# Two pairs of projections side by side in a hybrid attention, retention and linear-attention trunk

## The chip, the cores and the metric

The kernel runs on one core of a Trainium2 chip. The metric is the device time of one execution in microseconds; a kernel's time is the median of its runs. The core has five engines with instruction streams of their own: TensorE (PE; its weight loads are shown as PEld), VectorE (DVE), ScalarE (ACT), GpSimd (POOL) and SyncE (SP), which here only issues DMAs. Each runs its instructions in order and waits on semaphores for the others.

## The reference, cut to what matters

Two layers over 1024 tokens of width 1024, all in float32. A layer normalises the tokens, projects them once, runs three groups of heads beside each other, gates them and projects back:

```python
h = rms_norm(x, pre_gain) * (1.0 + scale) + shift
proj = h @ w_in
(aq, ak, av, ag, rq, rk, rv, rg, gq, gk, gv, gg, ga) = jnp.split(proj, IN_SPLITS, axis=-1)
...
a_out = sliding_window_attention(aq, ak, av, sinks) * jax.nn.silu(ag)
...
rq = apply_rotary(rq.reshape(B, S, RET_HEADS, RET_DK), positions, ret_freq)
rk = apply_rotary(rk.reshape(B, S, RET_HEADS, RET_DK), positions, ret_freq)
r = retention(rq, rk, rv.reshape(B, S, RET_HEADS, RET_DV))
r_out = rms_norm(r).reshape(B, S, RET_W) * jax.nn.silu(rg)
...
g = gated_linear_attention(...)
g_out = rms_norm(g, gla_norm_gain).reshape(B, S, GLA_W) * jax.nn.silu(gg)
y = jnp.concatenate([a_out, r_out, g_out], axis=-1) @ w_out
return x + gate * rms_norm(y, post_gain)
```

`rq`, `rk`, `rv` and `gv` are 256 columns wide each; `ak` and `av` are 128 each and lie next to each other, so the kernel treats them as one unit, `kv`, of 256.

## The kernel before, in words

**Tiles.** The tokens are eight tiles of 128; two tiles make a pair `p` (0 to 3), four a half `hf`. The columns of `w_in` and `w_out` are cut into units of 256 (`UNITS`): `gg` and `rg` (gates), `rq`, `rk`, `rv` (retention), `gqk` and `gv` (linear attention's queries with keys, and its values), `kv` (attention's keys and values), `aq0`, `aq1`, `ag0`, `ag1`, and `o0` to `o3` of the output.

**Precision.** Every float32 operand of a large product is held as two parts, a high part and the rest (`a` = 0 and 1). A product is three passes of eight matmuls over the 1024 rows (`PASSES`, L623; `accum`, L625): high by high, low by high, high by low. A projection of one tile by one unit is so 24 matmuls.

**Two shapes of projection.** `project` (L634) keeps a block of 128 tokens stationary and moves the 256 columns of one weight unit. `project_T` (L641) keeps 128 columns of weights stationary and moves 512 tokens, out of two pairs' token blocks that lie in two slots; the operand is made by `both` (L148), which describes two runs of 256 with one step between them. `y_half` (L1221) uses `both` for two weight units of the output in the same way.

**Memory.** Seven slots hold weights and token blocks in turn. `PLACE` (L53) says which unit goes to which slot in each layer, `TURNED` (L48) which units begin 48 elements into their slot, and `SW` (L51) where the blocks of layer 1's output product go. `load` (L520) fetches a unit in four chunks of 256 KB, one DMA each on SP's queue, into one of five staging buffers (`st`), and turns each chunk into its two parts: the high part by ACT or DVE, the rest by DVE, the last chunk's by POOL. A slot is written only when its last reader has finished. Other pools that matter below: eight 256-wide work tiles (`t1`), ten 512-wide ones (`t2`), two large ones (`mx`), three PSUM banks for projections (`mm`) and five for the rest (`aux`).

**The order of PE's work** is the order in which the program writes it. Projections are the trunk of that order. Everything else (cores of the heads, norms, the next layer's modulation) is written as jobs that yield a delay. The program keeps a planned clock, `clk`, which each matmul advances by its columns divided by 2400 (in us); between projections and inside `accum` it calls `pump`, which writes the steps of the jobs whose delay has passed. The delays are in the table `L` (L1691; a key with `@1` holds for layer 1): `rc1`, for example, is the time from a retention core's creation to its first transposes on PE. The other engines' order is left to the compiler's scheduler.

**The stages around the change.** In `layer` (L1480), after the gates, retention goes pair by pair: `rq` for two tiles, `rk` for two, `rv` for two. Each `rq` and `rk` tile is rotated by `ret_rot` (L1168), five DVE operations in `rotary` (L831) and one for the decay; each `rv` tile is evicted by ACT and creates its `ret_core` (L1174). A core transposes queries and keys on PE, evicts them by ACT, makes the scores, masks them on DVE, multiplies with the values and updates the state. After the last tile of each of these units, its slot's next unit is requested. Then comes linear attention: `gqk` in four units, `gv` pair by pair, each pair creating a `gla_core` (L1092), and `kv`, whose first pair stands between `gv`'s third and fourth pair and whose other pairs come after. `attn_kv` (L863) evicts the values and rotates and transposes the keys. Then follow attention's queries (`aq0`, `aq1`, with `attn_rot`, L875) and its gates (`ag0`, `ag1`).

The `pk`, `pm` of these functions are one `mm` bank each; a unit of 256 columns fills half of it.

Of the kernel before, what the change touches and what calls it, by code (L numbers as in the profile page):

```python
# [17 lines left out]
P = 128  # L18
# [29 lines left out]
TURNED = ("gqk", "aq0", "aq1", "ag0", "ag1")  # L48
TOKEN_AT, PLAIN_AT, TURNED_AT, OUT_AT, BLOCK_AT = 48, 0, 48, 0, 64
PLAIN = 2  # L50
SW = dict(W00=6, T1=3, W11=4, W10=5, T2=2, T3=0, T4=1)  # L51
TOK = ((1, 2, 3, 4), (3, 4, 0, 1))
PLACE = []  # L53
for _t, _w in zip(TOK, (0, 2)):
    PLACE.append(dict(gg=_w, rg=5, rq=6, rk=_w, rv=5, gqk=6, gv=_w, kv=5, aq0=6, aq1=_w, ag0=5, ag1=_w,
                      o0=_t[0], o1=_t[1], o2=5, o3=6))
# [37 lines left out]
def trunk(ctx: ExitStack, tc: tile.TileContext, ins, cst, out):  # L94
# [53 lines left out]
    def both(x, y):  # L148

        return bass.AP(x.tensor, x.offset, [x.ap[0], (y.offset - x.offset, 2), (1, 256)])  # L150
# [1329 lines left out]
    def layer(l):  # L1480
# [3 lines left out]
        def do_gates(name, p):  # L1484
            w = used(l, name)
            for t in (2 * p, 2 * p + 1):
                pg = mm()
                if name == "gg":
                    project(pg[:, 0:272], l, t, w, 272)
                    job(gla_logits(l, t, pg[:, 0:256], pg[:, 256:272]))  # L1490
                else:
                    project(pg[:, 0:256], l, t, w)
                    dma("ssr", srS[t], silu2(pg[:, 0:256]))
                pump()
            if p == NP_ - 1:
# [59 lines left out]
        def do_gv(p):  # L1555
            for t in (2 * p, 2 * p + 1):
                pm = mm()
                project(pm[:, 0:256], l, t, used(l, "gv"))
# [4 lines left out]
                pump()  # L1563
            if p == NP_ - 1:
                load(l, "aq1")

        def do_kv(p):
            if p == 0:
                new_kv()
            for t in (2 * p, 2 * p + 1):  # L1570
                pk = mm()
                project(pk[:, 0:256], l, t, used(l, "kv"))
                job(attn_kv(l, t, pk))
                pump()
# [116 lines left out]
L = {"sw1": 0.4, "ld1": 1.2, "ld2": 1.2, "ld1@1": 1.2, "ld2@1": 1.27, "swW00": 0.0, "swT1": 0.0, "swW11": 0.4, "swW10": 0.5, "tt1": 8.0, "tt2": 1.75, "tb1": 24.5, "tb2": 0.75, "pf3": 13.2, "pf1": 6.35, "pf2": 4.16, "mod1": 4.6, "mod2": 4.0, "mod3": 13.29, "mod4": 7.04, "mod5": 3.36, "mod6": 9.04, "pre1": 7.44, "kv1": 3.1, "kv2": 2.11, "aq1": 6.0, "aq7": 6.0, "ag1": 5.44, "aq2": 2.4, "aq6": 5.2, "aq3": 10.21, "aq4": 7.36, "aq5": 3.6, "hn1": 8.93, "hn2": 2.85, "gz1": 11.18, "gz2": 8.13, "gl1": 2.76, "gd3": 15.9, "gc1": 0.62, "gc2": 1.94, "gc3": 1.33, "gc4": 0.87, "gc6": 0.86, "gc5": 1.14, "rc1": 0.8, "rc2": 1.09, "rc3": 5.87, "rc4": 2.51, "fin1": 7.28, "lay1": 1.13, "gc4@1": 0.93, "mod2@1": 4.0, "mod3@1": 15.1, "mod5@1": 3.36, "mod6@1": 4.11, "pre1@1": 7.44, "kv1@1": 2.79, "kv2@1": 5.28, "aq1@1": 4.8, "aq7@1": 5.28, "ag1@1": 6.25, "aq2@1": 0.82, "aq6@1": 6.0, "aq3@1": 10.9, "aq4@1": 4.4, "aq5@1": 5.15, "hn1@1": 8.12, "hn2@1": 2.85, "gz1@1": 15.91, "gz2@1": 10.94, "gl1@1": 4.6, "gd3@1": 15.9, "gc1@1": 0.48, "gc2@1": 1.94, "gc3@1": 1.33, "gc6@1": 0.86, "gc5@1": 1.04, "rc1@1": 0.37, "rc2@1": 0.84, "rc3@1": 1.9, "rc4@1": 2.79, "fin1@1": 4.28, "lay1@1": 1.7}  # L1691
# [36 lines left out]
```

## Time and profile before

| | |
|---|---|
| runs | 1002.62, 1007.8 and 1005.75 us, median 1005.75 |
| profiled execution | 1000.26 us |
| its span, first to last instruction | 998.5 us |
| mean granted clock of TensorE | 0.987 of full |
| weights loaded out of `w_in` | 96 chunks of 256 KB |
| transposes on PE (L188), tiles of the work pool | 288 of 128 x 128 |

A page of the profile gives busy time by engine, the chain of waits that ended last, and groups of equal instructions by line and shape. In the timeline a row reads: start, length, engine, line, operation, output<-input, shapes, count; in square brackets stands how long the engine was idle before it and what ended that. A line of a helper stands for all its callers: L173 is every matmul, L188 every transpose, L157 every ACT copy, L162 most DMAs, L546 the low part of a weight chunk. `arena` is the memory of the slots. The end of a matmul is modelled; the start of the next one is what counts.

### The profile page before, as it was taken

Reading aid. Unit: us, or ns where it says so; the run is one execution under the profiler, and the core shown is the slowest. Engines: PE = TensorE matmul, PEld = TensorE weight load, DVE = VectorE, ACT = ScalarE, POOL = GpSimd, SP = SyncE. Lnnn points to the kernel's source line nnn. Section 1 sums busy time; section 2 is a strip of 40 time slices with the busy share of each in tenths; the row PEclk is TensorE's granted clock in tenths of the full one; section 3 lists DMA queues with packets and bytes.
Section 4 is the critical chain, followed back from the end, with each engine's and each line's share of the span. In section 5 each row is a group of like instructions: output and inputs, shape, how many; then the busy total and the mean of one; then the engine's idle time right before and its main releaser. Section 6 shows DMA issues by size and latency. Waiting matters only on the chain.

```text
span 998.5 us, 19629 instructions
## 1 busy us (share of the span) xinstructions
PE 961.3 (96%) x7133; PEld 825.5 (83%) x7133; DVE 690.5 (69%) x1698; ACT 409.6 (41%) x1152; POOL 236.0 (24%) x275
## 2 busy tenths in 40 slices
PE   5798999999999999999999999999999999999896
PEld 2598999888998777778889999998899877777675
DVE  3779856857767778664588285685666577676886
ACT  2476411324332556542356242123333267664231
POOL 2210101232330234330113010113332034555000
PEclk8899999999999999999999999999999999999998
DMA  9832613523326255668646151343132433487883
GB/s 315 296 114 79 186 48 88 161 89 101 110 81 188 79 154 155 203 192 259 228 150 203 49 175 38 106 136 116 41 107 85 127 90 123 131 247 242 262 268 136
DMA packets 129968, 148.76 MB, mean 149 GB/s; under 512 B 14112, under 2 KB 94284, under 8 KB 129872
## 3 DMA queue, kind: packets, MB, share of 16 engines
q1 hardware_dynamic: 124176, 137.96, 45.2%
q10 hardware_dynamic: 5696, 9.56, 2.5%
q8 instruction: 56, 0.92, 0.4%
q14 instruction: 40, 0.33, 0.1%
HBM read 109.20 MB, written 36.18 MB: 146 GB/s over the span
## 4 chain that ended last, share of the span: by engine, by line
PE 75%; DVE 10%; DMA 7%; ACT 3%; issue 3%; POOL 2%; SPq 1%; ACTq 0%; POOLq 0%; DVEq 0%
PE mm L173 56%; PE aux L173 14%; PE aux L188 4%; DMA st<-in_w_in_dram 2%; POOL sm L650 2%; DMA t<-mixF 1%; DMA xk<-in_x_dram 1%; DMA t<-in_x_dram 1%; DMA aoS<-t 1%; DMA a<-mixS 1%; DVE arena L546 1%; DVE arena L723 1%; ACT t L666 1%; DVE t L715 1%; SPq L162 1%
## 5 line engine op out<-in xcount | busy, mean ns | idle before, releaser
L173 PE MATMUL mm<-arena 128*128 128x256 f32 (+2 forms) x1824 | 299.5, 318 | 4.2 <-DVE t L1008 2.7
L173 PE MATMUL mm<-arena,arena 128*128 128x256 f32 (+2 forms) x1824 | 297.4, 316 | 0.3 <-DVE t L1008 0.3
L173 PEld LDWEIGHTS mm<-arena 128*128 128x128 f32 x1824 | 255.3, 191 | 28.4 <-issue 3.3
L173 PEld LDWEIGHTS mm<-arena,arena 128*128 128x128 f32 x1824 | 252.5, 188 | 23.9 <-issue 4.3
L650 POOL TENSOR_TENSOR sm<-sm,mhalf 128x1 f32<-128x1 f32 (+1 forms) x64 | 55.9, 874 | 347.3 <-DVE sm L649 334.9
L173 PE MATMUL mm<-arena,mx 128*128 128x512 f32 (+1 forms) x564 | 128.2, 383 | 1.4 <-ACT kept L1355 1.4
L173 PEld LDWEIGHTS mm<-arena,mx 128*128 128x128 f32 x564 | 101.6, 188 | 22.9 <-ACT kept L1355 1.8
L157 ACT ACTIVATE t<-aux 128x256 f32<-128x256 f32 (+2 forms) x124 | 55.9, 468 | 73.7 <-PE aux L188 62.5
L157 ACT ACTIVATE arena<-st 128x512 fp32r<-128x512 f32 x94 | 55.9, 626 | 51.2 <-PE mm L173 19.0
L546 POOL TENSOR_TENSOR arena<-st,arena 128x512 fp32r<-128x512 f32 x31 | 43.3, 1401 | 133.2 <-ACT arena L157 96.7
L945 POOL TENSOR_TENSOR smx<-smx,sm 128x512 f32<-128x512 f32 x32 | 36.4, 1138 | 124.2 <-DVE sm L944 114.2
L546 DVE TENSOR_TENSOR arena<-st,arena 128x512 fp32r<-128x512 f32 x77 | 59.1, 787 | 5.9 <-ACT arena L157 3.7
L941 ACT ACTIVATE smx<-smx,sm 128x129 f32<-128x129 f32 x128 | 49.9, 392 | 27.8 <-DVE sm L938 27.8
L188 PE MATMUL aux<-c_ident,t 128*128 128x128 f32 (+1 forms) x292 | 48.6, 284 | 7.8 <-DVE t L681 7.4
L375 DVE SCALAR_TENSOR_TENSOR acc<-st,c_act,acc 128x512 f32<-128x512 f32 x60 | 45.4, 757 | 14.1 <-DMA st<-in_w_mod_dram 13.6
L188 PEld LDWEIGHTS aux<-c_ident,t 128*128 128x128 f32 (+1 forms) x292 | 35.2, 145 | 15.0 <-DVE t L681 9.4
L989 ACT ACTIVATE t<-aux 128x256 f32<-128x256 f32 x32 | 12.3, 384 | 75.7 <-PE aux L173 72.2
L173 PEld LDWEIGHTS aux<-t,mx 32*128 32x128 f32 (+1 forms) x896 | 39.5, 187 | 3.8 <-issue 2.0
L713 ACT ACTIVATE t<-aux,mod,mod 128x128 f32<-128x128 f32 x68 | 25.7, 459 | 37.0 <-DVE t L1262 19.4
L173 PE MATMUL aux<-t,mx 32*128 32x32 f32 (+1 forms) x896 | 40.6, 272 | 0.0
L936 DVE COPY_PREDICATED smx<-c_curmask,aux 128x256 f32<-128x256 int32 x64 | 25.5, 447 | 16.0 <-ACT smx L157 13.0
L1262 DVE SCALAR_TENSOR_TENSOR t<-t,sm,t 128x512 f32<-128x512 f32 x32 | 24.0, 780 | 17.8 <-DMA t<-in_x_dram 11.5
(223 smaller groups left out, 1382.9 us busy)
## 6 DMA issues: line engine op xcount, KB each, us to landing
st<-in_w_in_dram SPq DMA_DIRECT2D x96, 256.0 KB, 3.1
st<-in_w_mod_dram SPq DMA_DIRECT2D x64, 256.0 KB, 2.8
st<-in_w_out_dram SPq DMA_DIRECT2D x52, 256.0 KB, 3.7
mx<-mixS SPq DMA_DIRECT2D x20, 512.0 KB, 4.9
mixS<-t SPq DMA_DIRECT2D x72, 128.0 KB, 3.1
wm<-in_w_mod_dram SPq DMA_DIRECT2D x12, 512.0 KB, 6.6
t<-in_x_dram SPq DMA_DIRECT2D x24, 256.0 KB, 4.9
t<-tabS SPq DMA_DIRECT2D x16, 256.0 KB, 3.8
```

Of the source, the lines that this page charges most:

```text
L157: A.activation(dst, src, AF.Copy)
L173: T.matmul(dst, lhsT, rhs, start=start, stop=stop)
L188: T.transpose(dst, src, idn)
L375: V.scalar_tensor_tensor(acc, wt, c_act[:, k:k + 1], acc, ALU.mult, ALU.add)
L546: e.tensor_tensor(lo, st, f(hi), ALU.subtract)
L650: G.tensor_tensor(r, r, mhalf[:, :w], ALU.pow)
L713: A.activation(hf[:, ks], at[kt], AF.Identity, scale=gain, bias=shift)
L936: V.copy_predicated(sv, curmask.unsqueeze(1).to_broadcast((P, 2, P)), pv[:, :, n // P - 1, :])
L941: A.activation(sm[:, h, :], sm[:, h, :], AF.Exp, bias=mx[:, h:h + 1], accum_out=sums[:, h:h + 1])
L945: eng("pn").tensor_tensor(sm[:, :, 0:128], sm[:, :, 0:128], rs.unsqueeze(2).to_broadcast((P, 4, P)), ALU.mult)
L989: A.activation(sq, po, AF.Square)
L1262: V.scalar_tensor_tensor(xt[j], yg[j], r, xt[j], ALU.mult, ALU.add)
```

## The change

A new function `project2` projects one tile by two units at once: the token block is stationary as before, and `both` makes one moving operand of 512 columns out of the two units, which must lie in the same arena. It is used for `rq` with `rk`, and for `gv` with `kv`.

For that the two units of a pair must be in memory at the same time. In retention a pair of tiles now begins with `rv` for both tiles; then each tile is projected by `rq` and `rk` in one product, both are rotated, and the tile's core is created, with a longer `rc1`. In linear attention `do_gkv` takes the place of `do_gv` and `do_kv`. The slots, and with them the loads, are given out anew: `gqk` is requested after the last `rv`, `gv` and `kv` after the last `rq` and `rk`, `aq1` after the last `gv` and `kv`. The four units of the pairs begin 48 elements into their slots.

```diff
-TURNED = ("gqk", "aq0", "aq1", "ag0", "ag1")
+TURNED = ("gqk", "aq0", "aq1", "ag0", "ag1", "rq", "rk", "gv", "kv")
...
-SW = dict(W00=6, T1=3, W11=4, W10=5, T2=2, T3=0, T4=1)
+SW = dict(W00=5, T1=3, W11=4, W10=6, T2=2, T3=0, T4=1)
...
-    PLACE.append(dict(gg=_w, rg=5, rq=6, rk=_w, rv=5, gqk=6, gv=_w, kv=5, aq0=6, aq1=_w, ag0=5, ag1=_w,
-                      o0=_t[0], o1=_t[1], o2=5, o3=6))
+    PLACE.append(dict(gg=_w, rg=5, rq=6, rk=5, rv=_w, gqk=_w, gv=5, kv=6, aq0=_w, aq1=5, ag0=6, ag1=_w,
+                      o0=_t[0], o1=_t[1], o2=6, o3=5))
...
+    def project2(l, t, u, v):
+        w0, w1 = used(l, u), used(l, v)
+        await_flag(("hT", l, t))
+        c = slice((t % 2) * P, (t % 2) * P + P)
+        h = hT[(l, t // 2)]
+        pm = mm()
+        accum(pm.rearrange("p (s n) -> p s n", s=2), lambda a, k: h[:, a, k, c],
+              lambda b, k: both(w0[:, b, k, 0:256], w1[:, b, k, 0:256]))
+        return pm
...
-                load(l, "rk" if name == "gg" else "rv")
+                load(l, "rv" if name == "gg" else "rk")
...
-            for name in ("rq", "rk", "rv"):
-                w = used(l, name)
-                for tt in range(2):
-                    t = 2 * p + tt
-                    pm = mm()
-                    project(pm[:, 0:256], l, t, w)
-                    src = pm[:, 0:256]
-                    if name == "rv":
-                        v = t1()
-                        copy("rv", v, src)
-                        job(ret_core(l, t, rr[("rq", tt)], rr[("rk", tt)], v))
-                    else:
-                        rr[(name, tt)] = ret_rot(t, src, qdec if name == "rq" else kdec)
-                    pump()
-                if last:
-                    load(l, {"rq": "gqk", "rk": "gv", "rv": "kv"}[name])
+            w = used(l, "rv")
+            for t in (2 * p, 2 * p + 1):
+                pm = mm()
+                project(pm[:, 0:256], l, t, w)
+                rr[t] = t1()
+                copy("rv", rr[t], pm[:, 0:256])
+                pump()
+            if last:
+                load(l, "gqk")
+            for t in (2 * p, 2 * p + 1):
+                pm = project2(l, t, "rq", "rk")
+                q, k = (ret_rot(t, pm[:, 256 * i:256 * i + 256], d) for i, d in enumerate((qdec, kdec)))
+                job(ret_core(l, t, q, k, rr[t]))
+                pump()
+            if last:
+                load(l, "gv")
+                load(l, "kv")
...
+        def do_gkv(p):
+            if p == 0:
+                new_kv()
             for t in (2 * p, 2 * p + 1):
-                pm = mm()
-                project(pm[:, 0:256], l, t, used(l, "gv"))
+                pm = project2(l, t, "gv", "kv")
                 vs[t] = t1()
                 copy("gv", vs[t], pm[:, 0:256])
                 if t % 2:
                     job(gla_core(l, p, qks[p], (vs[t - 1], vs[t])))
...
+                job(attn_kv(l, t, pm[:, 256:512]))
                 pump()
 
         do_gqk(0, 0)
         do_gqk(0, 1)
-        do_gv(0)
+        do_gkv(0)
         do_gqk(1, 0)
-        do_gv(1)
+        do_gkv(1)
         do_gqk(1, 1)
-        do_gv(2)
-        do_kv(0)
-        do_gv(3)
-        for p in range(1, NP_):
-            do_kv(p)
+        do_gkv(2)
+        do_gkv(3)
+        load(l, "aq1")
         load(l, "ag0")
...
-                    if l == DEPTH - 1 and g == 0:
+                    if l == DEPTH - 1 and g == 1:
                         sw_first("W00")
                     else:
-                        load(l, ("o3", "ag1")[g])
+                        load(l, ("ag1", "o3")[g])
...
-L = {... "rc1": 0.8, ... "rc1@1": 0.37, ...}
+L = {... "rc1": 7.0, ... "rc1@1": 6.8, ...}
```

More of the change, by code (lines that the diff above doesn't have):

```diff
@@ L148, in both @@
     def both(x, y):
+        assert x.tensor is y.tensor
         return bass.AP(x.tensor, x.offset, [x.ap[0], (y.offset - x.offset, 2), (1, 256)])
@@ L1553, in do_gqk @@
                 load(l, "aq0")
-        def do_gv(p):
+        def do_gkv(p):
+            if p == 0:
+                new_kv()
             for t in (2 * p, 2 * p + 1):
-                pm = mm()
-                project(pm[:, 0:256], l, t, used(l, "gv"))
+                pm = project2(l, t, "gv", "kv")
                 vs[t] = t1()
@@ L1562, in do_gv @@
                     job(gla_core(l, p, qks[p], (vs[t - 1], vs[t])))
[L1563 to L1573, printed above, removed]
+                job(attn_kv(l, t, pm[:, 256:512]))
                 pump()
@@ L1690 @@
 EN = {"shw0": "V", "shw1": "A", "shw2": "A", "shw3": "A", "slw0": "V", "slw1": "G", "slw2": "V", "slw3": "G", "sht2": "A", "sht3": "A", "sht4": "A", "slt2": "V", "slt3": "G", "slt4": "G", "sd": "V", "mh0": "A", "mh1": "A", "mh2": "A", "mh3": "A", "mf": "A", "ms0": "V", "ms1": "V", "ms2": "V", "ms3": "V", "yg0": "V", "yg1": "V", "ml0": "V", "ml1": "V", "ml2": "V", "ml3": "V", "mod0": "A", "mod1": "V", "qst": "S", "smh": "S", "sml": "S", "sm0": "S", "sm1": "S", "lao": "S", "sao": "S", "lmix": "S", "ssg": "S", "lsg": "S", "ssr": "S", "lsr": "S", "lx": "S", "sx": "A", "lw": "S", "lwm": "S", "whi0": "V", "whi1": "A", "whi2": "A", "whi3": "A", "wlo0": "V", "wlo1": "V", "wlo2": "V", "wlo3": "G", "xn0": "V", "xn1": "V", "hlo0": "V", "hlo1": "V", "rot0": "V", "rot1": "V", "rdec": "V", "kslo": "V", "qslo": "V", "vlo": "G", "kT": "A", "qT": "A", "sprev": "A", "pn": "G", "pf0": "A", "aoc": "A", "hng": "V", "mh": "A", "gso": "V", "mg": "V", "mgl": "V", "rT": "A", "rv": "A", "gv": "A", "gk": "A", "ak0": "V", "ak1": "V", "ak2": "V", "ak3": "V", "kd0": "G", "kd1": "G", "kd2": "G", "kx1": "G", "kx2": "G", "kx3": "V", "kx4": "V", "qb": "G", "stx": "V"}
-L = {"sw1": 0.4, "ld1": 1.2, "ld2": 1.2, "ld1@1": 1.2, "ld2@1": 1.27, "swW00": 0.0, "swT1": 0.0, "swW11": 0.4, "swW10": 0.5, "tt1": 8.0, "tt2": 1.75, "tb1": 24.5, "tb2": 0.75, "pf3": 13.2, "pf1": 6.35, "pf2": 4.16, "mod1": 4.6, "mod2": 4.0, "mod3": 13.29, "mod4": 7.04, "mod5": 3.36, "mod6": 9.04, "pre1": 7.44, "kv1": 3.1, "kv2": 2.11, "aq1": 6.0, "aq7": 6.0, "ag1": 5.44, "aq2": 2.4, "aq6": 5.2, "aq3": 10.21, "aq4": 7.36, "aq5": 3.6, "hn1": 8.93, "hn2": 2.85, "gz1": 11.18, "gz2": 8.13, "gl1": 2.76, "gd3": 15.9, "gc1": 0.62, "gc2": 1.94, "gc3": 1.33, "gc4": 0.87, "gc6": 0.86, "gc5": 1.14, "rc1": 0.8, "rc2": 1.09, "rc3": 5.87, "rc4": 2.51, "fin1": 7.28, "lay1": 1.13, "gc4@1": 0.93, "mod2@1": 4.0, "mod3@1": 15.1, "mod5@1": 3.36, "mod6@1": 4.11, "pre1@1": 7.44, "kv1@1": 2.79, "kv2@1": 5.28, "aq1@1": 4.8, "aq7@1": 5.28, "ag1@1": 6.25, "aq2@1": 0.82, "aq6@1": 6.0, "aq3@1": 10.9, "aq4@1": 4.4, "aq5@1": 5.15, "hn1@1": 8.12, "hn2@1": 2.85, "gz1@1": 15.91, "gz2@1": 10.94, "gl1@1": 4.6, "gd3@1": 15.9, "gc1@1": 0.48, "gc2@1": 1.94, "gc3@1": 1.33, "gc6@1": 0.86, "gc5@1": 1.04, "rc1@1": 0.37, "rc2@1": 0.84, "rc3@1": 1.9, "rc4@1": 2.79, "fin1@1": 4.28, "lay1@1": 1.7}
@@ new lines @@
+L = {"sw1": 0.4, "ld1": 1.2, "ld2": 1.2, "ld1@1": 1.2, "ld2@1": 1.27, "swW00": 0.0, "swT1": 0.0, "swW11": 0.4, "swW10": 0.5, "tt1": 8.0, "tt2": 1.75, "tb1": 24.5, "tb2": 0.75, "pf3": 13.2, "pf1": 6.35, "pf2": 4.16, "mod1": 4.6, "mod2": 4.0, "mod3": 13.29, "mod4": 7.04, "mod5": 3.36, "mod6": 9.04, "pre1": 7.44, "kv1": 3.1, "kv2": 2.11, "aq1": 6.0, "aq7": 6.0, "ag1": 5.44, "aq2": 2.4, "aq6": 5.2, "aq3": 10.21, "aq4": 7.36, "aq5": 3.6, "hn1": 8.93, "hn2": 2.85, "gz1": 11.18, "gz2": 8.13, "gl1": 2.76, "gd3": 15.9, "gc1": 0.62, "gc2": 1.94, "gc3": 1.33, "gc4": 0.87, "gc6": 0.86, "gc5": 1.14, "rc1": 7.0, "rc2": 1.09, "rc3": 5.87, "rc4": 2.51, "fin1": 7.28, "lay1": 1.13, "gc4@1": 0.93, "mod2@1": 4.0, "mod3@1": 15.1, "mod5@1": 3.36, "mod6@1": 4.11, "pre1@1": 7.44, "kv1@1": 2.79, "kv2@1": 5.28, "aq1@1": 4.8, "aq7@1": 5.28, "ag1@1": 6.25, "aq2@1": 0.82, "aq6@1": 6.0, "aq3@1": 10.9, "aq4@1": 4.4, "aq5@1": 5.15, "hn1@1": 8.12, "hn2@1": 2.85, "gz1@1": 15.91, "gz2@1": 10.94, "gl1@1": 4.6, "gd3@1": 15.9, "gc1@1": 0.48, "gc2@1": 1.94, "gc3@1": 1.33, "gc6@1": 0.86, "gc5@1": 1.04, "rc1@1": 6.8, "rc2@1": 0.84, "rc3@1": 1.9, "rc4@1": 2.79, "fin1@1": 4.28, "lay1@1": 1.7}
```

## The prediction

> **What bounds the kernel now.** I read the page's busy times and its chain of waits first, then the stretches by window, then the waits of PE.
>
> ```profile
> span 998.5 us, 19629 instructions
> PE 961.3 (96%) x7133; PEld 825.5 (83%) x7133; DVE 690.5 (69%) x1698; ACT 409.6 (41%) x1152; POOL 236.0 (24%) x275
> PE 75%; DVE 10%; DMA 7%; ACT 3%; issue 3%; POOL 2%; SPq 1%; ACTq 0%; POOLq 0%; DVEq 0%
> ```
>
> TensorE is busy for 96% of the span and holds 75% of the chain. The two stages that the change touches, by window (columns: length, then busy time of PE, PEld, DVE, ACT, POOL, the granted clock, DMA share, GB/s):
>
> ```profile
> 100.00:120.00 20.00, 20.00 (x172) 19.92 (x171) 19.68 (x55) 7.39 (x18) 2.43 (x2) 1.00 0.65 201
> 120.00:140.00 20.00, 20.00 (x176) 19.46 (x176) 13.04 (x44) 5.52 (x10) 2.18 (x2) 1.00 0.17 52
> 195.00:200.68 5.68, 2.43 (x14) 1.75 (x12) 2.44 (x6) 2.29 (x5) 0.73 (x1) 1.00 0.86 249
> 200.68:204.85 4.17, 4.17 (x16) 3.32 (x17) 0.76 (x2) 0.00 (x0) 0.53 (x1) 0.59 0.73 217
> 650.00:670.00 20.00, 19.89 (x172) 19.40 (x173) 18.23 (x54) 6.25 (x14) 4.95 (x4) 1.00 0.43 121
> ```
>
> In retention PE is full, so a microsecond of matmul saved there is a microsecond of time, unless a wait takes its place. VectorE (DVE) has room in the middle (13.04 of 20) and hardly any at the two ends of the stage (19.68 and 18.23 of 20). PE idles once per layer, at the join of retention and linear attention:
>
> ```profile
> 199.24 0.63 ACT L157 ACTIVATE arena<-st 128x512 fp32r<-128x512 f32 x1 [2.85 <-DMA st<-in_w_in_dram]
> 199.78 0.85 ACT L157 ACTIVATE t<-aux 128x256 fp32r<-128x256 f32 x2
> ```
> ```profile
> 200.68 1.20 PE L173 MATMUL aux<-t 64*128 64x128 f32 x8 [3.26 <-ACT t L157]
> ```
> ```profile
> 673.97 0.63 ACT L157 ACTIVATE arena<-st 128x512 fp32r<-128x512 f32 x1 [3.80 <-DMA st<-in_w_in_dram]
> ```
> ```profile
> 675.13 0.72 PE L173 MATMUL aux<-t 64*128 64x128 f32 x8 [1.31 <-ACT t L157]
> ```
>
> ScalarE (ACT) stands at the conversion of a weight chunk whose DMA has not landed; the eviction of retention's transposes is queued behind it; PE waits 3.26 us in layer 0 and 1.31 us in layer 1. After the longer one the clock is 0.59 for 4.17 us, another 4.17 x 0.41 = 1.7 us. The Trainium skill ("TensorE: Matmul & The Clock Gate", Part 1) says that an idle window of about 3.4 us halves the clock; the pair of 3.26 and 1.31 us agrees with it.
>
> **The change part by part.** First the matmuls. Per layer, 8 tokens' tiles x 24 matmuls x 2 pairs = 384 pairs of 256-column matmuls become 384 of 512 columns; in both layers 768 for 1536. The cadence of each shape is read from long pieces of the chain, time over count:
>
> ```profile
> 308.94 16.35 PE mm L173 x72
> 575.12 13.31 PE mm L173 x113
> 779.97 15.45 PE mm L173 x68
> 963.35 16.32 PE mm L173 x72
> ```
>
> The piece at 575.12 is gates, queries and keys, all 256 columns: 13.31/113 = 117.8 ns. The other three are 512 columns wide (the first and third move two token blocks, 256 columns each, a slot apart): 227.1, 227.2 and 226.7 ns. So side by side saves 2 x 117.8 - 227.2 = 8.4 ns a pair, and 768 x 8.4 = **6.4 us**. Almost all of a matmul's time here is columns, and these stay; only the part per instruction is halved.
>
> The Trainium skill (the same page, "Back-to-back issue gap") gives columns/2.4 + 2.5 ns. By that a pair would save 2.5 ns and the sum be 1.9 us. The rows stand above it, 117.8 against 109.2 and 227.2 against 215.8 ns, and the excess hardly grows with the columns, so the row decides.
>
> New to the trace is the negative step between the two weights of a pair (queries in slot 6, keys in slot 5), with a token block stationary. Its bounds are no saving at all (235.6 ns, twice the 256-column row) and the 226.7 ns row (6.8 us); I take 227.2, the nearest row in shape. The 768 weight loads that go lie beside matmuls and count nothing. The 48-element offset of four units moves addresses only; the piece at 308.94 already has both operands at that offset.
>
> Second, retention's **order**. Values come first for two tiles, then queries with keys tile by tile, and the core's transposes follow 7.0 planned us (`rc1`) after a pair's projection instead of 0.8. The planner books 213 ns for a 512-column matmul that takes 227, so 7.0 becomes 7.5 us. In that time VectorE has to do two rotations. One without company, and one in the full window:
>
> ```profile
> 125.20 0.42 DVE L839 TENSOR_TENSOR t<-mm,sincos 128x256 f32<-128x256 f32 x1 [0.80 <-PE mm L173]
> 126.46 0.43 DVE L1171 TENSOR_TENSOR t<-t,c_qdec 128x256 f32<-128x256 f32 x1
> ```
> ```profile
> 107.67 0.42 DVE L839 TENSOR_TENSOR t<-mm,sincos 128x256 f32<-128x256 f32 x1
> 110.29 0.41 DVE L1171 TENSOR_TENSOR t<-t,c_qdec 128x256 f32<-128x256 f32 x1
> ```
> ```profile
> 102.16 0.99 PE L173 MATMUL mm<-arena,arena 128*128 128x256 f32 x7
> ```
>
> Alone it is 126.89 - 125.20 = 1.7 us, so 3.4 for two, 4.1 us inside the margin. In the full window the projection begun at 102.16 ended near 105.4 (24 x 0.1178 and 0.4 of other work), and its rotation at 110.70, 5.3 us late; with the second rotation 7.0 us, still 0.5 inside. So I count zero. If that cover goes, PE stands at the transposes, with all projections behind them; the rotations due next and the `mm` banks follow. Values are also held some 12 us longer in the pool of eight 256-wide tiles; the cover is that cores now come evenly, one per tile.
>
> Third, the **weights**. At the start values take the keys' old place in slot 0 and keys the values' old place in slot 5, loads requested at the same points as before:
>
> ```profile
> 99.83 1.30 POOL L546 TENSOR_TENSOR arena<-st,arena 128x512 fp32r<-128x512 f32 x1 [22.59 <-ACT arena L157]
> 107.92 1.29 POOL L546 TENSOR_TENSOR arena<-st,arena 128x512 fp32r<-128x512 f32 x1 [6.78 <-ACT arena L157]
> ```
> ```profile
> 589.66 0.68 DVE L546 TENSOR_TENSOR arena<-st,arena 128x512 fp32r<-128x512 f32 x1
> ```
>
> Slot 0 is complete at 101.13, values start at 102.16: 1.0 us to spare. Slot 5 is complete at 109.21; keys' low halves are read in the last third of their first tile, 102.16 + 48 x 0.1178 + 16 x 0.227 = 111.5 at the earliest: 2.3 us to spare. In layer 1 the last low half came at 590.34 and would be wanted about 589; it stood behind rotations that now come later, so from 0 to 1.3 us, and I take 0.
>
> At the join, slots 5 and 6 come free together, when the last query-key tile ends, and both weights of the next pair go there: eight chunks, one 256 KB DMA each on SP, through five staging buffers.
>
> ```profile
> st<-in_w_in_dram SPq DMA_DIRECT2D x96, 256.0 KB, 3.1
> ```
>
> Five can land ahead; three must be issued after the first conversions. Three landings in a row are 9.3 us; the cover is two `gqk` units of 24 matmuls (48 x 0.2272 = 10.9 us) and what is left of two retention cores. So the projection itself waits for nothing. But those three chunks stand on ACT's queue ahead of the last two cores' evictions, as one chunk does now. Bounds: the present waits vanish (-6.3 us, with the clock) or grow (the slower rival below); I take them as unchanged.
>
> `aq1` is requested six 256-column projections later than now (6 x 24 x 0.1178 = 17 us); its four landings, 12.4 us in a row, lie beside the 48 matmuls of `aq0` (10.9 us) and the last core; uncovered they would cost the difference, 1.5 us. `ag1` and `o3` change places, and in layer 1 `W00` moves by one unit; both are wanted about 40 us later. All of it counts zero.
>
> Fourth, linear attention's last cores move beside the attention queries, whose split writes the two `mx` buffers that the cores hold:
>
> ```profile
> 282.52 0.38 PE L188 MATMUL aux<-c_ident,mx 128*128 128x128 f32 x2
> 295.56 1.00 PE L173 MATMUL aux<-t,mx 128*128 128x64 f32 x8
> 304.63 1.10 PE L173 MATMUL mm<-arena,arena 128*128 128x512 f32 x4
> ```
> ```profile
> 322.63 1.15 ACT L854 ACTIVATE mx<-t 128x512 fp32r<-128x512 f32 x2 [3.21 <-DMA t<-t]
> ```
>
> The last core's first step followed the last value projection at 282.52 and its last read of a buffer was 13-14 us later (296.56). The first split comes 18.0 us after the queries begin (304.63 to 322.63). If the queries begin where the core does, 4 us are left: zero again. The key-value work itself (rotation, split, transposes) is the same; it is only spread over the stage.
>
> The **sum**: -6.4 us and nothing beside it. The profiled execution took 1000.26 us, 1.76 around its span of 998.5; it becomes 993.9. The median of the three runs, 1005.75, is 5.5 us above that execution; I take the saving off the median: **999.4 us**.
>
> **The rivals.** Half a per cent, 5.0 us, is about what a measurement of this kernel can tell from no change.
>
> *The joins close* (999.4 - 6.3 = 993 us). Both waits of 3.26 and 1.31 us and the slow clock go, because the last cores now come 7.5 us after their projection, when the chunk has landed. Against it: three chunks then have to land at that place instead of one.
>
> *Retention's rotations come late* (1004 us). VectorE at 19.68 and 18.23 of 20 us, and only 0.5 us inside the margin in the full window. If half of the 16 cores wait 0.6 us, that is 4.8 us, and 1.6 are left of the saving; also where values held longer keep a rotation from its buffer. For it: the in-order PE and the full window; against: 9 to 13 of 20 us in the middle of the stage, and at the start two value projections (5.7 us) that, in the changed order, give VectorE nothing.
>
> *No saving* (1005.75 us). The reverse step or the token block as the stationary operand makes the 512-column matmul cost twice the 256-column one. Three rows at 226.7 to 227.2 ns speak against it; none has that very shape.
>
> *The page's constant*: a matmul's fixed part is smaller than the rows' slope says, as if the excess were the clock's or the memory's and went with the columns. From rows: with the fixed part at a third of 8.4 ns, 768 x 2.8 = 2.2 us, 1003.6. I count it with the last one. The Trainium skill's 2.5 ns would be this case; the rows do not bear it out.
>
> *Slower: the doubled load at the join* (1017 us). Place: ACT's queue at the end of retention, in both layers. The chunk issued there took from 193.91 to 199.16 to land:
>
> ```profile
> 193.91 5.25 DMA st<-in_w_in_dram
> ```
>
> If ACT stands through two such landings, 10.5 us a layer, with the evictions of cores 6 and 7 behind, PE loses 2 x 10.5 - 3.26 - 1.31 = 16.4 us more than now, and in layer 1 also the 1.7 us of slow clock: 18.1 - 6.4 = +11.7. It decides from 11.4 us of added waiting (6.4 + 5.0). For it: the two slots come free at one moment, the DMA share was 0.86 there. Against it: five of eight chunks can be staged before.
>
> **How the numbers follow.** The forecast 0.40 (its own range 996 to 1002: the saving by its bounds, the joins by 2 us either way); the joins close 0.15; rotations late 0.22; no or a third of the saving 0.08; slower 0.15. Faster by over 0.5%: the first by 0.35 (some of its range is under 5 us), the second 0.15, 0.02 of the third: 0.52. Slower: 0.12 of the last, 0.03 of the third: 0.15. The rest, 0.33, is no change. The range 992 to 1009 holds the first four cases and leaves out most of the slower one.
>
> **What would show it.** In the groups by shape the 256-column rows fall from 2304 to 768 matmuls and 768 of 512 columns appear; the chain's long pieces in retention then read 227 ns a matmul (235 would prove the reverse step right). PE waits at L188 on DVE L1171 mean late rotations; at the join, PE's wait on ACT L157 behind an `arena<-st` and the clock after it decide between the forecast, the closing and the slower rival. A PE wait on `arena` conversions at the first query-key tile or the first value-pair tile would show weights late. The prediction is wrong if the time is outside 996 to 1002 with the cadence at 227, or if the new waits together exceed 2 us.

## The result, and the profile after

The changed kernel takes 1030.36 us (median of 4, 1028.86 to 1038.14) where the kernel before took 1006.77 (median of 4): ratio 1.0272, 95% interval 1.0235 to 1.0308. It is slower by 23.6 us; the forecast was 999.4. The profiled executions differ by 28.6 us of span, more than the medians, because the profiled one of before (1000.26 us) was faster than each of its four runs. The page of the kernel after, its span and PE's line:

```profile
span 1027.1 us, 18042 instructions
PE 977.9 (95%) x6365; PEld 799.7 (78%) x6365; DVE 691.9 (67%) x1698; ACT 405.8 (40%) x1152; POOL 237.9 (23%) x275
```

PE has 768 matmuls fewer than the 7133 of before, as the change says, and more busy time, not less. The cause shows first in the view of the cores, whose last column is the mean granted clock. Before:

```profile
core 0: 998.5 us, clock 0.987
```

After:

```profile
core 0: 1027.1 us, clock 0.968
```

**The saving is there.** In the timeline of PE after (start, length, operation), a piece of 28 matmuls of queries with keys, 512 columns, with the reverse step between the two weights:

```profile
115.81 6.52 PE L174 MATMUL mm<-arena,arena 128*128 128x512 f32 x28
122.17 2.05 PE L174 MATMUL mm<-arena 128*128 128x256 f32 x16
```

(122.17 - 115.81)/28 = 227.1 ns, against the 227.2 taken and 235.6 for no saving.

**Where the time came from.** Three marks split the span: the first matmul of linear attention's values, the evictions of `gqk`, and the tanh on attention's gates (first and last start of a line's instructions in a layer). In the timeline of before, first the values in layer 0, then `gqk` in layer 1, then the gates of layers 0 and 1:

```profile
214.40 2.64 PE L173 MATMUL mm<-arena 128*128 128x256 f32 x21
...
L1550 ACT ACTIVATE t<-mm x4: 379/384/384, 681.6 to 703.9; 128x256 f32<-128x256 f32 x4
...
L1597 ACT ACTIVATE t<-mm x8: 576/586/599, 368.5 to 425.5; 128x512 f32<-128x512 f32 x8
...
L1597 ACT ACTIVATE t<-mm x8: 577/584/602, 842.6 to 909.6; 128x512 f32<-128x512 f32 x8
```

And after:

```profile
210.63 3.01 PE L174 MATMUL mm<-arena,arena 128*128 128x512 f32 x12
...
L1562 ACT ACTIVATE t<-mm x4: 377/381/390, 687.4 to 715.1; 128x256 f32<-128x256 f32 x4
...
L1598 ACT ACTIVATE t<-mm x8: 576/580/600, 371.8 to 431.7; 128x512 f32<-128x512 f32 x8
...
L1598 ACT ACTIVATE t<-mm x8: 576/582/602, 869.1 to 935.2; 128x512 f32<-128x512 f32 x8
```

Up to the joint projection the kernel after is 3.8 us ahead (214.40 to 210.63). At the last gate of layer 0 it is 6.2 us behind (425.5 to 431.7): 10.0 us lost. At layer 1's first eviction of `gqk` it is 5.8 us behind, so 0.4 came back in between. At the last gate of layer 1 it is 25.6 us behind: another 19.8 lost. The output stage adds 3.0: PE waits 4.6 us there once for ScalarE (L1366; 1.4 us before), and 2.1 us of its work go to a low clock right behind. So 30 us are lost between the joint projection and the end of attention's gates, in the two layers together.

What PE waited for there (engine, operation, releaser: us in total, times, longest), layer 0 between 200 and 340 us:

```profile
PE aux L189 <- DVE mx L1146: 2.6, 3, 1.4
PE aux L189 <- ACT t L1130: 1.5, 1, 1.5
PE aux L189 <- DVE t L855: 1.0, 1, 1.0
```

Layer 1 between 690 and 830 us:

```profile
PE aux L189 <- DVE mx L1146: 2.1, 1, 2.1
PE aux L174 <- DVE t L993: 2.0, 2, 1.2
```

The waits shown are 9.2 us together (before, 0.6 us in the same stages, beside the stall at the join). Most of the rest is the clock. By windows in layer 1 (length, then busy time of PE, PEld, DVE, ACT, POOL, granted clock, DMA share, GB/s):

```profile
788.00:792.00 4.00, 2.24 (x59) 1.96 (x58) 4.00 (x11) 1.90 (x8) 1.48 (x2) 0.92 0.59 171
792.00:796.00 4.00, 3.70 (x9) 2.59 (x9) 1.46 (x7) 0.28 (x1) 0.00 (x0) 0.50 0.80 250
796.00:800.00 4.00, 4.00 (x60) 3.83 (x60) 1.67 (x4) 0.66 (x4) 0.00 (x0) 0.50 0.01 2
800.00:804.00 4.00, 4.00 (x10) 3.04 (x10) 0.95 (x4) 0.68 (x3) 0.00 (x0) 0.50 0.41 131
804.00:808.00 4.00, 4.00 (x27) 3.36 (x26) 0.40 (x2) 0.38 (x1) 0.00 (x0) 0.88 0.54 164
```

A busy PE at clock 0.50 does half the work: the 8 matmuls of 512 columns that begin at 792.42 take until 796.11, 461 ns each instead of 227. So this stretch alone costs some 6.3 us (3.70, 4.00 and 4.00 x 0.50, 4.00 x 0.12). What stands ahead of it, in PE's timeline (the bracket is the idle time before, and its releaser):

```profile
787.62 0.38 PE L189 MATMUL aux<-c_ident,mx 128*128 128x128 f32 x2
...
789.81 0.44 PE L189 MATMUL aux<-c_ident,t 128*128 128x128 f32 x2
792.30 0.47 PE L189 MATMUL aux<-c_ident,t 128*128 128x128 f32 x1 [2.05 <-DVE mx L1146]
792.42 3.76 PE L174 MATMUL mm<-arena,arena 128*128 128x512 f32 x8
```

and in VectorE's of the same moment:

```profile
790.02 0.28 DVE L850 TENSOR_TENSOR t<-mm,sincos 128x128 f32<-128x128 f32 x1
...
790.62 0.21 DVE L855 TENSOR_TENSOR t<-t,tr 128x64 f32<-128x64 f32 x1
790.75 1.28 DVE L547 TENSOR_TENSOR arena<-st,arena 128x512 fp32r<-128x512 f32 x2
791.96 0.88 DVE L1146 COPY_PREDICATED mx<-c_mask,aux 128x128 f32<-128x128 int32 x4
```

At 787.62 a `gla_core` begins: two transposes, one half of its scores (56 small matmuls of 32 columns in the trace; I call such a half a burst), a head norm's two transposes, and at 792.30 the one transpose of attention's keys. That one is there because the keys now come out of the same projection as the values whose last tile starts the core. VectorE is full (4.00 of 4.00): the keys' rotation runs from 790.02 to 790.83, two weight conversions follow, then the copies (L1146) that empty the score banks. The transpose waits for one of these copies, not for its own operand, which had been ready since 790.83: by the order in which the program takes the five `aux` banks, four hold scores and the fifth the head norm's transposes. From 787.6 to 792.4 there is no wide matmul, and the clock falls.

### The profile page after: what moved, and what is told of

The parts are those of the page before. It is cut to its first block, busy times and chain, and to the rows that moved or that the text cites. A ratio compares the mean times of both kernels' runs of the same rounds, so it can differ in the third digit from the quotient of the medians.

```text
span 1027.1 us, 18042 instructions
## 1 busy us (share of the span) xinstructions
PE 977.9 (95%) x6365; PEld 799.7 (78%) x6365; DVE 691.9 (67%) x1698; ACT 405.8 (40%) x1152; POOL 237.9 (23%) x275
## 5 line engine op out<-in xcount | busy, mean ns | idle before, releaser
L174 PE MATMUL mm<-arena,arena 128*128 128x512 f32 (+2 forms) x1440 | 304.2, 364 | 0.3 <-DVE t L1019 0.3
L174 PE MATMUL mm<-arena 128*128 128x512 f32 (+2 forms) x1440 | 296.7, 358 | 4.9 <-DVE t L1019 3.4
L174 PEld LDWEIGHTS mm<-arena,arena 128*128 128x128 f32 x1440 | 236.3, 194 | 39.6 <-issue 3.2
L174 PEld LDWEIGHTS mm<-arena 128*128 128x128 f32 x1440 | 232.2, 192 | 42.7 <-DVE t L1019 4.3
L174 PE MATMUL mm<-arena,mx 128*128 128x512 f32 (+1 forms) x564 | 130.4, 388 | 5.0 <-ACT kept L1366 4.6
L547 POOL TENSOR_TENSOR arena<-st,arena 128x512 fp32r<-128x512 f32 x31 | 46.0, 1486 | 127.2 <-ACT arena L158 73.1
L189 PE MATMUL aux<-c_ident,t 128*128 128x128 f32 (+1 forms) x292 | 48.7, 286 | 19.8 <-DVE t L692 10.0
L376 DVE SCALAR_TENSOR_TENSOR acc<-st,c_act,acc 128x512 f32<-128x512 f32 x60 | 49.8, 830 | 18.5 <-DMA st<-in_w_mod_dram 16.3
L547 DVE TENSOR_TENSOR arena<-st,arena 128x512 fp32r<-128x512 f32 x77 | 57.3, 767 | 2.5 <-ACT arena L158 1.3
L174 PEld LDWEIGHTS aux<-t,mx 32*128 32x128 f32 (+1 forms) x896 | 44.5, 211 | 8.2 <-issue 4.4
L174 PE MATMUL aux<-t,mx 32*128 32x32 f32 (+1 forms) x896 | 45.8, 294 | 2.0 <-DVE t L993 2.0
L174 PEld LDWEIGHTS aux<-kT,mx 64*128 64x128 f32 x384 | 24.8, 185 | 11.5 <-issue 5.9
```

Source lines behind the costliest of these rows:

```text
L174: T.matmul(dst, lhsT, rhs, start=start, stop=stop)
L189: T.transpose(dst, src, idn)
L376: V.scalar_tensor_tensor(acc, wt, c_act[:, k:k + 1], acc, ALU.mult, ALU.add)
L547: e.tensor_tensor(lo, st, f(hi), ALU.subtract)
```

## The experiments

The theories: (1) the loss is in linear attention, where the joint projection puts the keys' work between the cores' bursts, and the waits and small matmuls there lose the clock; (2) 512-column matmuls themselves; (3) retention's order spoils linear attention; (4) weight slots and loads. All ratios are to the kernel before on the same chip; its median was 1003.2 to 1006.8 us from chip to chip, so a difference between two experiments is safer by the ratios than by the medians. The edits show only what changes; ... stands for code not shown. For each kernel I summed over windows of 4 us PE's busy time x (1 - clock), and the idle time, in the two linear-attention stages (200 to 344 and 680 to 832 us; us of each, clock + idle):

```
kernel                                     span    ratio [95%]              layer 0      layer 1
before                                    998.5                            1.4 + 1.1    0.0 + 0.3
after                                    1027.1   1.0272 [1.0235, 1.0308]   5.0 + 5.7   13.3 + 4.8
keys' transposes later                   1021.9   1.0147 [1.0081, 1.0212]   5.1 + 1.0    9.9 + 3.9
retention's pair alone                   1005.2   1.0035 [1.0012, 1.0058]   0.0 + 1.4    1.7 + 1.3
order of after, 256 columns              1035.4   1.0319 [1.0288, 1.0351]  18.0 + 9.1    1.7 + 2.5
six small banks                          1031.6   1.0331 [1.0278, 1.0383]   1.6 + 4.1    1.6 + 3.2
transposes held back                     1017.4   1.0127 [1.0095, 1.0160]   6.7 + 3.2    3.1 + 2.5
held back and spread                     1014.3   1.0110 [1.0085, 1.0136]   3.3 + 3.2    4.5 + 5.6
held back, halves cut in two             1022.2   1.0238 [1.0192, 1.0285]   1.6 + 5.7    1.5 + 5.7
before, score halves together            1045.6   1.0430 [1.0402, 1.0459]  19.0 + 9.4   13.4 + 7.0
before, values first in the last pair    1010.2   1.0105 [1.0074, 1.0135]   3.1 + 2.6    1.2 + 1.4
```

(The 1.4 of before in layer 0 is the clock after its stall at the join; the stall itself lies ahead of 200 us but for 0.7.)

**The keys' transposes later.**

```
-        yield lat("kv1", l)
+        yield lat("kv1", l) + (10.0 if t % 2 else 0.0)
```

> The kernel after, with one edit: the key transposes of every odd tile (attn_kv) come due 10 planned us later, so that they no longer fall between the score blocks of gla_core. Theory 1 (these transposes wait on VectorE's COPY_PREDICATED for an aux bank, and the stretches of small matmuls with such a wait in them lose the TensorE clock): most of the 28 us come back; the waits of 2.6 and 2.1 us at the transposes in the two linear-attention stages go, the stretches at granted clock 0.50 become fewer than three, the time is 1000 to 1012 us. Theory 2 (the 512-column matmuls themselves cost more), theory 3 (retention's order pushes work into linear attention) and theory 4 (weight slots and their loads): it stays within 5 us of 1030.

1021.42 us (1010.08 to 1023.98). The waits behind L1146 are gone from both stages, and 9 us by the medians came back (12.6 by the ratios), not the 18 or more that theory 1 wrote down; (2) to (4), which had it unmoved, fall for this part. What stayed: in layer 1 the scores still wait behind store_mix (1.9 us, L993), and the clock still falls. In layer 0 it falls with hardly a wait. Timeline of PE, and the windows (PE busy, clock, DMA share, GB/s):

```profile
294.84 3.94 PE L174 MATMUL mm<-arena 128*128 128x512 f32 x16
298.62 0.38 PE L189 MATMUL aux<-c_ident,mx 128*128 128x128 f32 x2
...
299.60 1.38 PE L174 MATMUL aux<-t,mx 32*128 32x32 f32 x41 [0.25 <-DVE t L1005]
...
301.24 1.21 PE L174 MATMUL mm<-arena 128*128 128x512 f32 x4
302.28 0.60 PE L189 MATMUL aux<-c_ident,t 128*128 128x128 f32 x2
```
```profile
300.00:304.00 4.00, 4.00 (x55) 0.79 0.56 156
304.00:308.00 4.00, 4.00 (x59) 0.50 0.74 209
308.00:312.00 4.00, 4.00 (x11) 0.50 0.53 160
```

Between 298.6 and 302.3 PE stood 0.25 us and did four wide matmuls; the rest is 32-column scores and a few transposes. So a long wait is not needed for the clock to go. The same program lost different amounts from run to run: its four times, 1010.08, 1019.24, 1023.59 and 1023.98 us, go with mean clocks of 0.986, 0.976, 0.969 and 0.969, and the trace is that of the third.

**Retention's pair alone.** Linear attention in the order and width of before:

```
-        do_gkv(0) ... do_gkv(3)
+        do_gv(0) ... do_gv(2); do_kv(0); do_gv(3); do_kv(1) ... do_kv(3)
```

> The kernel after, with only retention's queries and keys side by side: linear attention's values and attention's keys and values are projected apart again, at 256 columns and in the order of the kernel before; the slots are those of after. Theory 1 (the loss sits in the linear-attention half): 996 to 1002 us, that is 1005.75 less 3.2 us for 384 pairs and some 3 to 5 us for the joins between retention and linear attention, which showed no stall in the trace after. Theory 2 (512-column matmuls cost more): 1015 to 1020, half of the loss. Theory 3 (retention's order pushes work into linear attention): over 1020. Theory 4 (slots and loads): about 1030.

1007.45 us: not the loss of theories 2 to 4, and not the gain of theory 1 either, but 0.35% slower. Linear attention is as quiet as before (4.4 us in both layers together, 28.8 after), so the loss of the change is the other half's: 1.0272 against 1.0035, some 23 us. Retention's own gain is given back in small pieces. One is a wait of PE that before doesn't have, in layer 1's gates:

```profile
PE mm L174 <- DVE t L1019: 1.9, 1, 1.9
```

Others are stretches with a low clock: 0.70 in the window from 548 us (gates), 0.57 in that from 720 us (linear attention), and 0.76 in that from 940 us (output stage, behind a wait of 3.1 us at L1366).

**The order of after, at 256 columns.**

```
-        accum(pm.rearrange(...), ..., lambda b, k: both(w0[:, b, k, 0:256], w1[:, b, k, 0:256]))
+        for i, w in enumerate((u, v)):
+            project(pm[:, 256 * i:256 * i + 256], l, t, used(l, w))
```

> The kernel after with the order of its units kept, but each side-by-side projection made as two projections of 256 columns, one after the other, into the two halves of the same bank. Theory 1 (order and collisions, not width): still slow, 1025 to 1040 us, the 6.4 us of the width lost again, or a few us less where the two halves, which end 2.8 us apart, spread linear attention's work. Theory 2 (width): back to 1000 to 1008. Theories 3 and 4 (order of retention, slots): 1030 to 1040.

1036.59 us, 6.2 above the kernel after by the medians (4.7 by the ratios, 8.3 by the spans). The width saves about what was forecast, as far as a spread from 4.7 to 8.3 us can say: the lost time in the table differs by 2.5 us between these two as well. The order makes the loss without the width, so theory 2 falls. Theories 3 and 4 had this time in their range too; it is the run with retention's pair alone that speaks against them. Here the waits are for head norms, ahead of the scores in layer 0:

```profile
PE aux L174 <- DVE t L989: 4.9, 3, 1.7
```

**Six small banks.**

```
-MMB = 3
+MMB = 2
```

(one value in the line of the buffer counts: two PSUM banks for projections, six for the rest)

> The kernel after, with six PSUM banks for the small work (aux) and two for the projections (mm), where it has five and three. Theory 1a (the waits in linear attention are for an aux bank: one score half takes four, its kbn transposes one, so a head norm's or a key's transposes that stand beside them hold the bank that the scores need until VectorE's copies have read it): the waits at the transposes behind the COPY_PREDICATED line and at the scores behind store_mix's subtract go, about 7 us of idle, and with them part of the stretches at clock 0.50; 1005 to 1020 us, less what two mm banks cost elsewhere (a wait at the 512-column projections behind ACT or VectorE, which the trace would name). Theory 1b (the waits are for VectorE's results themselves, the rotated keys): the waits stay with the same releasers, 1025 to 1040.

Linear attention's lost time falls from 28.8 to 10.5 us; no wait behind L1146 is left there. That is theory 1a: those transposes waited for a bank. A wait of 1.7 us behind store_mix and one of 1.0 for the rotated keys stay. But with two projection banks PE now waits elsewhere, above all in the gates: 4.7 us once at 100 us (L1019), and between 345 and 680 us:

```profile
PE mm L174 <- DVE t L1019: 5.1, 2, 3.0
```

The sum is 1035.17 us, outside the 1005 to 1020 expected.

**Transposes held back.** A value `hold` is set while a core waits for its decays, makes its operands and issues its scores; attention's keys and the head norms wait for its end:

```
+        while clk[0] < hold[0]:
+            yield 0.4
```

(behind `kv1` in attn_kv and `hn1` in head_norm_gate)

> The kernel after, with one rule more: while a gla_core waits for its decays, makes its operands and issues its two score halves, and for 1 planned us behind, the transposes of attention's keys and of the head norms aren't issued; they come right behind. Theory 1: no wait behind store_mix's subtract or COPY_PREDICATED before or between the scores; stretches without a matmul of 256 or 512 columns are under 3 us; no 8 us at clock 0.50; 998 to 1008 us, below the run with the key transposes alone delayed (1021). Theory 2 to 4: 1020 to 1030. If the two score halves with their transposes are by themselves enough to lower the clock, it stays at 1010 to 1024 with no waits.

1016.33 us: 14 of the 23.6 us came back, but not 998 to 1008. It is close to the expectation's last case: the waits are short (5.7 us in both layers), yet the clock still falls:

```profile
232.00:236.00 4.00, 3.78 (x29) 0.70 0.01 4
236.00:240.00 4.00, 4.00 (x48) 0.50 0.00 0
240.00:244.00 4.00, 4.00 (x13) 0.52 0.10 33
```

This one followed a wait of 1.5 us for ScalarE, which evicts the core's own transposes (L1136) behind the exponentials of the decays.

**Held back and spread.** The same with `gc3` 1.33 -> 3.2, so that 16 wide matmuls stand between the two score halves.

> As the run with the transposes held back, with the planned distance between the two score halves raised from 1.33 to 3.2 planned us, so that 16 wide matmuls (3.6 us) stand between them where 8 stood. If the clock is lost by dense stretches of small matmuls and not by the waits alone: no stretch at clock 0.50 in linear attention and 996 to 1004 us. If the waits alone decide: the same as the run with the transposes held back, within 3 us.

1014.70 us, within 3 us of the last, which the expectation gave to the waits: the distance between the halves alone does not decide. Its worst place is again waits in a burst, the longest 2.09 us for an `aux` bank in which a core's outputs stood until their head norm had read them (L1008).

**The kernel before, its score halves together.** No other edit than

```
-"gc3": 1.33, "gc3@1": 1.33
+"gc3": 0.0, "gc3@1": 0.0
```

> The kernel before, with one number changed: the planned distance between gla_core's two score halves is 0 instead of 1.33 planned us, so that no projection stands between them (7 to 14 matmuls of 256 columns did). No width, no slot and no other order is changed. Theory of the clock (a stretch of about 4 us that holds only score matmuls, transposes and a wait lowers the granted clock to 0.50 for 10 us or so): the second halves wait 1 to 2 us for aux banks behind COPY_PREDICATED, some of the eight cores are followed by a stretch at 0.50, and the time is 1015 to 1030 us, of which the waits alone are 8 to 14. If the clock were lost by the joint projection itself: only the waits, no stretch at 0.50 in linear attention, 1011 to 1018 us.

1047.22 us, 4.3% slower than the kernel before and above the 1015 to 1030 expected. Waits rise by 12.6 us over the span and the clock's share by 32.6 (from 1.4 to 34.0, the same sums from 100 us to PE's last matmul); together 45.2 of the 47.1 us of span. Layer 0's waits and two of the stretches:

```profile
PE aux L173 <- ACT t L1119: 4.8, 2, 3.2
```
```profile
284.00:288.00 4.00, 4.00 (x36) 0.50 0.10 36
...
308.00:312.00 4.00, 4.00 (x25) 0.50 0.17 58
312.00:316.00 4.00, 4.00 (x24) 0.50 0.01 3
```

With no unit side by side, the same clock loss appears, and larger. What the kernel before rested on was the projections between its score halves. This run alone doesn't part the bursts from the waits, since both grew.

**Held back, each half cut in two.**

```
+            yield 0.5   # between 12 and 16 score matmuls, and behind the kbn transposes
```

> The run with the transposes held back, with each score half cut in two and its kbn transposes apart from it: 0.5 planned us are given at each cut, so that four 512-column matmuls of the joint projection (0.9 us) stand between 12 and 16 score matmuls. Theory of the clock: no stretch without a wide matmul is over 2.2 us, nothing at 0.50 in linear attention, 1002 to 1009 us (the held-back run lost 10 us of its 1016 to low clock there). If the remaining loss is in VectorE's order or in the attention queries that now stand beside the last gla_core: 1012 to 1018 us, with the clock at 1.00.

The clock holds: only 3.1 us lost to it in both layers, and in the place where the held-back kernel fell to 0.50

```profile
234.00:238.00 4.00, 4.00 (x44) 1.00 0.02 4
238.00:242.00 4.00, 4.00 (x48) 1.00 0.00 0
```

The theory of the clock stands in that; its time, 1002 to 1009, does not: 1027.65 us. The cuts have a price. Timeline of PE:

```profile
235.84 0.87 PE L175 MATMUL aux<-t,mx 32*128 32x32 f32 x24
236.64 1.20 PE L175 MATMUL mm<-arena,arena 128*128 128x512 f32 x4
237.77 0.87 PE L175 MATMUL aux<-t,mx 32*128 32x32 f32 x24
...
238.80 2.12 PE L175 MATMUL mm<-arena,arena 128*128 128x512 f32 x8
```

Four wide matmuls take 1.13 us from start to start (236.64 to 237.77) where 4 x 0.2271 = 0.91 are due: 0.22 us. The small ones of this half take 0.80 and 1.03 us (235.84 to 236.64, 237.77 to 238.80), where an uncut half at full clock takes 1.69 (kernel after, 289.34 to 291.03): another 0.14. Two halves of four cores in two layers make 16 such cuts, 5.8 us at 0.36; waits grow by 5.7 us against the held-back kernel, and the clock gives 6.7 back. That makes 4.8 us, and so far are the two spans apart (1017.4 and 1022.2). The medians are 11.3 us apart; the held-back kernel's trace is its slowest run and this one's its fastest.

Of the waits, most are at attention's first scores, behind the split of its queries:

```profile
PE aux L175 <- DVE mx L867: 5.2, 4, 2.2
```

With the conversion of the high parts (L866, 1.3 us) this place costs 6.5 us, against 2.4 in the held-back kernel, 0.4 in the kernel after and nothing before. So the expectation's other case, attention's queries beside the last core, holds in part.

**Values first in the last pair, in the kernel before.**

```
-            for name in ("rq", "rk", "rv"):
+            for name in ("rv", "rq", "rk") if last else ("rq", "rk", "rv"):
```

(with 6 planned us more ahead of that pair's cores)

> The kernel before, all at 256 columns, with one order changed: in retention's last pair of tiles the values are projected first and the queries and keys behind them, and the last two ret_core come due 6 planned us later; nothing of linear attention is changed. If the 4 us that the retention half of the change gained at the join between the stages come from the order alone (the last cores leave the front of ScalarE's queue, where a weight load's wait held their copy), the stall of 3.26 us with its low clock at 200 to 204 us and that of 1.31 us in the second layer go, and the time is 0.994 to 0.998 of the kernel before. If the gain needs the 512-column pairs, or is given back in linear attention as it was in the run of the retention half alone, it is within 0.3%.

1013.48 us, 1.05% slower, which neither case had. The stall of 3.26 us in layer 0 is gone, as expected; in its place stand 0.8 us in layer 0 and, in layer 1:

```profile
PE aux L173 <- ACT t L157: 2.9, 1, 2.9
PE aux L188 <- DVE t L1171: 2.4, 1, 2.4
```

The old stall (1.31 us in layer 1) grew, and rotations came late (L1171). A new wait of 2.2 us in layer 0's linear attention (L982, at 224 us) has a low clock behind it. With this delay the gain at the join can't be had by that order alone. No version here beats the kernel before.

## Why the prediction was wrong

The *matmul* term held: 227.1 ns against 227.2. The time between the two widths in the same order, 6.2 us by the medians, is near the 6.4 too, but with a spread of 4.7 to 8.3 that is partly luck. The Trainium skill ("TensorE: Matmul & The Clock Gate", "Back-to-back issue gap") gives a fixed part of 2.5 ns a matmul, and an estimate from it was 1.9 us; the runs bear that out neither in the cadence nor in the time.

*Retention's order* held as forecast: PE never waits for the last step of a rotation in the kernel after (L1171 before, L1182 after). One wait of 1.7 us stands at the rotary tables (L461, at 112 us), which had not been named.

*The weights* held: no wait on a conversion at the first tile of either pair. What I missed of them is where their conversions run: two (L547) stood in VectorE's queue ahead of the score banks at 790.75.

*The joins* closed, which was a rival (0.15) and not the forecast: window 200 to 220 after has clock 1.00 and a full PE. The stall and its clock (5.0 us) with the 192 pairs of that layer (1.6) less the 1.7 at the tables would be 4.9; measured are the 3.8 us at the joint projection.

*Linear attention* is the step that failed: "The key-value work itself (rotation, split, transposes) is the same; it is only spread over the stage." It is the same work, but it isn't spread. In the kernel before, attention's keys and values of three of four pairs came behind the last value projection, away from the first three cores; side by side they come due 3 planned us after the tile that starts a core, between its score halves. I checked only the buffers that the cores share with the queries (4 us left; 0.4 us of waits there in the kernel after), not the five `aux` banks, of which one score half takes four, nor VectorE's queue. Measured: 10.0 and 19.8 us. Taking the keys' transposes out of the bursts brought 9 us by the medians (12.6 by the ratios), the head norms' as well 14 (14.6).

The second omission is the clock. I read it once, after the stall of 3.26 us, and gave it a price only there. The Trainium skill ("TensorE: Matmul & The Clock Gate", Part 1) speaks of an idle window of about 3.4 us; by that, no wait here would have mattered, since the longest in linear attention is 2.05 us. The rows say otherwise: 5.0 and 13.3 us of PE's work were lost to the clock in the two stages after, behind three bursts with waits of 1.2 to 2.05 us beside them, and in an experiment behind one with 0.25. My pair of 3.26 and 1.31 us, which agreed with the page, had no burst in it and so was no test of this. The same section calls the window free-running, with a spread from run to run; that agrees with the mean clocks, 0.962 to 0.975 in the runs of the kernel after and 0.969 to 0.986 with the keys' transposes later.

The *slower rival* had its sign and the wrong place: ScalarE's queue at the join, 1017 us. That place got better. The remaining chance for slower, 0.15, and a range ending at 1009 came from pricing only mechanisms that the trace of before already showed as waits.

What stays open: clock and idle together account for 30.5 us more than before from 100 us to PE's last matmul (20.4 + 22.9 against 1.4 + 11.4), less 6.4 for the width 24.1, of the 28.6; 4.5 us are not placed. Nor did the runs show what makes one burst lose the clock and another keep it, nor what a kernel would take whose last core alone stood away from attention's queries.

## What to carry to other kernels

Joining two projections moves every consumer of the second to the moment of the first; before pricing the matmuls saved, lay the joined consumers out against the bursts that the first one starts, and count banks and VectorE's microseconds there. A stretch of some 4 us that holds mostly small matmuls was a risk to the clock here even where PE looked busy, and the wide projections between them were not filler but what kept the rate. In a schedule tuned to the last wait, a saving of half a per cent is smaller than what a shift of the schedule can cost: both edits that left linear attention's order alone, retention's pair and the values first in its last pair, came out slower than the kernel before.

## What the runs showed of the hardware

The granted clock fell to 0.50 for some 9 us (303 to 312 us) behind a stretch with no idle time of PE over 0.25 us (keys' transposes later, 298.6 to 302.3 us), filled with 32-column matmuls, transposes and four wide matmuls. Yet no threshold can be read off: in the kernel after, 283.4 to 287.3 us holds no wide matmul and a wait of 1.43 us, and the clock stayed at 1.00. Four 512-column matmuls put into a run of 32-column ones cost 0.36 us of PE time beyond both (held back, halves cut in two, 235.84 to 238.80 us).
